# A matmul with a decayed running sum: one set of w's rows by another queue, ScalarE's order in the opening, and one PSUM bank

## The chip, the core and the metric

The kernel runs on one core of a Trainium2 chip. The core has TensorE (PE, matrix products into PSUM), VectorE (DVE), ScalarE (ACT), GpSimd (POOL) and SyncE (SP), and 16 DMA engines that all its DMA queues share. Each engine takes its instructions in the order in which the program gives them. The metric is device time in microseconds, the median over runs.

## The reference

x is [16, 2048, 1024], w is [1024, 1024], decay has 1024 values, all float32:

```python
xw = x @ w
out[:, 0, :] = xw[:, 0, :]
for t in range(1, S):
    out[:, t, :] = decay[None, :] * out[:, t - 1, :] + xw[:, t, :]
```

So there is one large product, and then along the sequence a linear recurrence for each batch and column.

## The kernel before

**Tiling.** The 16 sequences are cut into 64 chunks of 512 positions, and two neighbouring chunks make a group. The 1024 output columns are cut into 8 blocks of 128. The outer loop runs over groups, the inner one over blocks; one pass of the inner loop is a *slot*. Slots 0 to 7 are chunks 0 and 1 with blocks 0 to 7, slots 8 to 15 are chunks 2 and 3, and so on. A slot is 16 products of 128x128 with 128x512: k = 0 to 7 (the eight parts of the depth), for each of two chunks. Its result is two PSUM banks, columns on partitions and time along the free axis.

**PSUM.** There are eight banks. Three pairs, called `ps` 0 to 2, go round: slots 0, 1, 2 take them, then slots 4, 5, 6, then 7, 8, 9. Two single banks, `spare` and `spare1`, are used by slot 3, and after that not before the last group. A slot can only write its pair when the slot before on the pair has been emptied: slot 9 waits for slot 6.

**After the product** a slot takes one of two ways. Three of four are "paired": ScalarE copies the whole PSUM tile to SBUF (`copy`, line 183, a 128x1024 copy) and makes the decayed half of it (`odd`, line 169, `h<-ps`); GpSimd adds the two (`join`, line 196); VectorE scans half as many steps (line 201); ScalarE decays the result (`even`, line 169, `h<-so`) and GpSimd fills in the other half (`fill`, line 246). In the others VectorE scans PSUM directly (line 221). VectorE then transposes (line 258), and SyncE stores the result (line 282).

**x** is loaded by GpSimd's queue as bf16 (line 105), 32 rows at a time in four quadrants of a chunk, transposed by VectorE (`turn`, line 115) into `xw`, and put in order by a copy (`part`, line 123) into `xt`. A chunk's turn writes `xw`; its two ScalarE copies are called X (depth parts k = 0 to 3) and Y (k = 4 to 7).

**w** comes in four parts, (h, e): h is the half of the output columns, e says even or odd depth parts k. Part (0,0) is loaded as float32 by SyncE and ScalarE; the three others by GpSimd as bf16, four DMAs each, one per quadrant (`load_w`, line 299): U0 is part (0,1), U1 is (1,0), U2 is (1,1). A part has four row sets m = 0 to 3, and the row set m of part (h, e) is depth part k = 2m + e. The loaded rows are then copied into the stationary layout `wsb` (`settle`, line 306), one row set at a time: item number 8h + 4e + m. W is a settling by VectorE and w one by ScalarE.

**The order of the opening is written out by hand** in `agenda`, a list of letters with a number; key -99 stands ahead of slot 0, and the other keys follow the products of that slot. An engine's order is the order of its letters. p, g, z, j are copy, odd, zero and join of a slot; S is its scan; h, c, k are even, fill and the saving of its last column; B is the transpose back; L loads the next quadrant of x; T, X, Y turn and order a chunk; E, F, G do it for pieces of chunks 0 and 1; M loads them; D and d prepare decay and its square; K keeps TensorE going. So `p2` is ScalarE's copy of slot 2's tile, `w12` to `w15` are ScalarE's settling of part (1,1), and `j2` is GpSimd's join of slot 2.

In the opening the products of slots 0 to 3 are interleaved: for chunk 0 first the even k, then the odd ones. In slots 4 to 7 the even k come first too. Slots 8 and 9 are computed together: for chunk 2 slot 8's eight products, then slot 9's eight, and then the same for chunk 3, which reads `xw` directly. The pair of slot 9 is called `nexts`. The line numbers of the profile are those of this kernel:

Of the kernel before, what the change touches and what calls it, by code (L numbers as in the profile page):

```python
# [9 lines left out]
FP32 = mybir.dt.float32  # L10
# [4 lines left out]
def _ap(ap_obj: bass.AP, new_ap, extra_offset=0):  # L15
    return dataclasses.replace(
        ap_obj,
        ap=[list(p) for p in new_ap],
        offset=ap_obj.offset + extra_offset,
    )  # L20
# [5 lines left out]
def kernel(  # L26
# [26 lines left out]
    nc = tc.nc  # L53
    pin = tc.keep_in_program_order
    B, S, D = x.shape
    assert w.shape == (D, D)

    NQ = 4
    P = 32
    CQ = D // NQ  # L60
    K = CQ // P
    M = K // 2
    TL = 512
# [3 lines left out]
    CH = D // 2  # L67
    CR = CH // NQ

    const = ctx.enter_context(tc.tile_pool(name="const", bufs=1))  # L70
    sb = ctx.enter_context(tc.tile_pool(name="sb", bufs=1))
    psp = ctx.enter_context(tc.tile_pool(name="psp", bufs=1, space=bass.MemoryType.PSUM))
# [3 lines left out]
    def ring(pool, name, count, shape, dtype=FP32):  # L76
        i = turns[name] = turns.get(name, -1) + 1
        return pool.tile(shape, dtype, name=f"{name}{i % count}")

    def quad(q):  # L80
        return slice(q * P, (q + 1) * P)
# [7 lines left out]
    dec = const.tile([128, K], FP32, name="dec")  # L89
# [9 lines left out]
    xt_of = {}  # L99
# [25 lines left out]
    def matmul(ps, n, k, xt, t0=0, t1=TL, start=0, pairs=None):  # L125
        if pairs is None:
            rhs = xt[:, k // 2, k % 2, t0:t1]
        else:
            rhs = pairs[:, k // 2, t0 // P:t1 // P, :, k % 2].rearrange("p j i -> p (j i)")
        lhs = wsb[:, k, n].rearrange("p q i -> p (q i)")  # L130
        pin(nc.tensor.matmul(  # L131
            out=ps[:, t0:t1] if ps.shape[1] >= t1 else ps,
            lhsT=lhs,
            rhs=rhs,
            start=(k == 0 and t0 == start),
            stop=(k == K - 1),
        ))
# [3 lines left out]
    class Tile:  # L141
# [22 lines left out]
                self.held = sb.tile([128, 2 * TL + 2], FP32, name=f"so{self.turn % 4}")  # L164
            return self.held

        def decayed(self, src):
            h = ring(sb, "h", 4, [128, TL])[:, 0:self.T // 2]
            pin(nc.scalar.activation(  # L169
                out=h, in_=src, func=mybir.ActivationFunctionType.Copy,  # L170
                scale=dec[:, self.n:self.n + 1]))
            return h

        def pair(self):
            if self.paired:
# [4 lines left out]

        def copy(self):
            self.xs = sb.tile([128, 2 * TL], FP32, name=f"xs{self.lot % 3}")[:, 0:self.T]
            pin(nc.scalar.copy(out=self.xs, in_=self.ps))  # L183

        def odd(self):
            self.g = self.decayed(self.ps[:, 0:self.T:2])

        def zero(self):
            if self.prev is None:
# [8 lines left out]
        def scan(self):  # L198
            T, n, so = self.T, self.n, self.so
            if self.paired:  # L200
                pin(nc.vector.tensor_tensor_scan(  # L201
                    out=so[:, 3:T + 2:2],
                    data0=squares[-1][:, n:n + 1].to_broadcast([128, T // 2]),
                    data1=self.xs[:, 1:T:2],
                    initial=0.0 if self.prev is None else self.prev,
                    op0=ALU.mult,
                    op1=ALU.add,
                ))
            else:
                parts = self.ps if isinstance(self.ps, tuple) else (self.ps,)  # L210
                size = T // len(parts)
                for i, ps in enumerate(parts):
                    self.run(ps, i * size, size)

        def run(self, ps, t, size):
# [75 lines left out]
    size = M * CH  # L291
# [2 lines left out]
             (1, 0): room[1][:, 0:size // 2].bitcast(BF16),  # L294
             (1, 1): room[1][:, size // 2:size].bitcast(BF16)}

    def load_w(queues, h, e):
        for i, q in enumerate((0, 2, 1, 3)):
            pin(queues[i % len(queues)].dma_start(  # L299
                out=stage[h, e][quad(q)].rearrange("p (m d) -> p m d", m=M),  # L300
                in_=_ap(w, [[2 * D, P], [2 * P * D, M], [1, CH]],
                        (q * CQ + e) * D + h * CH)))

    def settle(h, e, m, copy):
        src = stage[h, e][:, m * CH:(m + 1) * CH]
        pin(copy(out=wcols[:, 2 * m + e, h],  # L306
                 in_=src.rearrange("p (q r i) -> p q r i", q=NQ, r=R)))

    idle = const.tile([128, TL], BF16, name="idle")
    spare = ring(psp, "spare", 1, [128, TL])  # L310
# [18 lines left out]
    for q in range(NQ):  # L329
        pin(nc.sync.dma_start(  # L330
            out=rows[q * P:q * P + R],
# [9 lines left out]
        spin(3 if q < NQ - 1 else 2, gates[q])  # L341

    def load_part(i):
        load_w((nc.gpsimd,), *((0, 1), (1, 0), (1, 1))[i])

    def part_one(i, copy):
        part(i // 8, copy, i % 4, i % 4 + 1, *halves[i // 4 % 2])
# [65 lines left out]
    def turn_and_load(c):  # L413
# [38 lines left out]
        "L": lambda i: load(*loads.pop(0)) if loads else None,  # L452
    }
    agenda = {
        -99: "M0 M1 U0 M2 M3 U1 U2 w0 W1 w2 W3 K0 K1 K2 K3 E0 E1 G0 E2 G1 E3 F2 G3 E4 E5 G4 E6 G5 E7 F6 G7 W4 w5 W6 W7 D E8 E9 G8 E10 G9 E11 F10 G11 E12 L E13 G12 L E14 G13 E15 L F14 G15",
        0: "p0 z0 W8 W9 W10 W11",
        1: "g0",
        2: "L S1 L",
        3: "p2 z2 L g2 j0 S3 w12 w13 L w14 L w15 k1",
        4: "j2 B1 d k3",  # L460
        5: "p4 L S0 L g4 S2 L k0 h0 j4 B3 h2",
        6: "k2 c0 T2 c2 p5 g5 B0 L X2 L",
# [85 lines left out]
    for step, (g, n) in enumerate(slots):  # L548
        T = TL * len(g)
        left = step - len(slots)  # L550
        if n % R == 0:
            ns, nj = range(n, n + R), T // P
            if left == -2 * R:
                outlets = [Outlet(ns, H, half) for half in range(2)]
            else:
                pieces = 1 if left < -7 * R else 2 if left < -6 * R else nj // H
                outlets = [Outlet(ns, nj, pieces=pieces)]
        if left == -R:
            outlets = []
        if step == 0:  # L560
            heads = [ring(psp, "ps", 3, [128, T]) for _ in range(3)]
            firsts = [ps[:, 0:TL] for ps in heads] + [spares[0]]
            seconds = [ps[:, TL:T] for ps in heads] + [spares[1]]
            for j0, j1 in halves:
                for k in range(0, K, 2):
                    for i in range(R):
                        matmul(firsts[i], i, k, xt_of[0], j0 * P, j1 * P, pairs=xw_of[0])
            for k in range(1, K, 2):
                for i in range(R):
                    matmul(firsts[i], i, k, xt_of[0])  # L570
            for k0 in range(0, K, 2):
                for i in range(R):
                    for k in (k0, k0 + 1):
                        matmul(seconds[i], i, k, xt_of[1], 0, H * P,
                               pairs=xw_of[1] if k0 < 4 else None)
            for i in range(R):
                for k in range(K):
                    matmul(seconds[i], i, k, xt_of[1], H * P, TL, H * P,
                           pairs=xw_of[1] if i < 2 else None)
        if step < R:  # L580
            ps = heads[n] if n < 3 else tuple(spares)
        else:
            if step == K + 1:
                ps = nexts
            elif len(g) == 2 or n % R < 3:
                ps = ring(psp, "ps", 3, [128, T])
            else:
                ps = ring(psp, "spare", 1, [128, TL])
            todo = [(k, l) for k in range(K) for l in range(len(g))]
            if step < K:  # L590
                todo.sort(key=lambda kl: kl[0] % 2)
            elif step == K:
                todo = []
                nexts = ring(psp, "ps", 3, [128, T])
                for l in range(len(g)):
                    for i, both in enumerate((ps, nexts)):
                        for k in range(K):
                            matmul(both[:, l * TL:(l + 1) * TL], n + i, k, xt_of.get(g[l]),
                                   pairs=xw_of[g[l]] if g[l] in (3,) else None)
            elif step == K + 1:  # L600
                todo = []
            if left == -1:
                ps = tuple(both[:, t:t + TL // 2] for t, both in zip(
                    (0, TL // 2), (ps, ring(psp, "ps", 3, [128, TL]))))
                blocks += [bank("spare1", 1), bank("ps", 3)]
                for t, half in zip((0, TL // 2), ps):
                    for k in range(K):
                        matmul(half, n, k, xt_of[g[0]], t, t + TL // 2, t)
                    if not t:
                        cross((1,), (0, 1))  # L610
                todo = []
            for k, l in todo:
                matmul(ps[:, l * TL:(l + 1) * TL], n, k, xt_of[g[l]])
        tiles.append(Tile(g, n, ps, outlets))
        do = agenda.get(step, agenda.get(left) if left >= -20 else None)
        if do is None:
            do = usual(step)
        else:
            do = do.split()
            if left == -20:  # L620
                do = rest(step) + do
        perform(do)
# [29 lines left out]
```

## Time and profile before

| | us |
|---|---|
| median of 3 runs | 904.99 (904.58 to 905.26) |
| span of the profiled execution, first to last instruction | 903.1 |
| median less span | 1.9 |
| TensorE busy (matmul) | 891.9, 99% of the span |
| VectorE busy | 825.6, 91% |
| ScalarE busy | 686.1, 76% |
| GpSimd busy | 657.1, 73% |
| granted TensorE clock, mean over the span | 1.000 |

In the answers of the trace, PE is TensorE's products and PEld its loads of the stationary operand. A line of a timeline has start, duration, engine, line, operation, what is written and read, shapes and a count; a bracket gives the idle time before it and what ended it. Neighbouring instructions of one kind are merged, so a line with x4 is four instructions. A matmul's record is longer than its share of TensorE, because products are pipelined: the distance from start to start is what one costs. Some matmul records are missing from the trace, so a step of two lengths is a missing record and no wait. A DMA's time to landing runs from its issue until all 16 engines have written their part.

### The profile page before, as it was taken

Reading aid. Unit: us, or ns where it says so; the run is one execution under the profiler, and the core shown is the slowest. Engines: PE = TensorE matmul, PEld = TensorE weight load, DVE = VectorE, ACT = ScalarE, POOL = GpSimd, SP = SyncE. Lnnn points to the kernel's source line nnn. Section 1 sums busy time; section 2 is a strip of 40 time slices with the busy share of each in tenths; the row PEclk is TensorE's granted clock in tenths of the full one; section 3 lists DMA queues with packets and bytes.
Section 4 is the critical chain, followed back from the end, with each engine's and each line's share of the span. In section 5 each row is a group of like instructions: output and inputs, shape, how many; then the busy total and the mean of one; then the engine's idle time right before and its main releaser. Section 6 shows DMA issues by size and latency. Waiting matters only on the chain.

```text
span 903.1 us, 12050 instructions
## 1 busy us (share of the span) xinstructions
PE 891.9 (99%) x4119; PEld 411.1 (46%) x4201; DVE 825.6 (91%) x632; ACT 686.1 (76%) x955; POOL 657.1 (73%) x755
## 2 busy tenths in 40 slices
PE   8999999999999999999999999999999999999998
PEld 5444444444444444444444444444444444444444
DVE  4999998999999999999998999999999999999998
ACT  4889867777877877878778778777787787787743
POOL 7888678777767768777677687777777776876632
PEclk9999999999999999999999999999999999999999
DMA  9999999999999999999999999999999999999858
GB/s 191 194 215 217 230 217 220 215 237 255 246 249 257 247 260 253 245 235 231 224 235 227 223 230 229 231 230 225 229 232 226 232 232 221 229 227 215 184 143 232
DMA packets 403182, 204.77 MB, mean 227 GB/s; under 512 B 9392, under 2 KB 402096, under 8 KB 403120
## 3 DMA queue, kind: packets, MB, share of 16 engines
q1 hardware_dynamic: 265808, 134.77, 61.0%
q0 software_dynamic: 137024, 68.70, 56.6%
q8 instruction: 33, 0.54, 0.2%
q10 hardware_dynamic: 288, 0.52, 0.2%
q14 instruction: 29, 0.24, 0.1%
HBM read 138.42 MB, written 134.22 MB: 302 GB/s over the span
## 4 chain that ended last, share of the span: by engine, by line
PE 94%; DMA 2%; POOL 1%; issue 1%; DVE 1%; ACT 0%; DVEq 0%; POOLq 0%
PE ps L131 94%; DMA xb<-in_x_dram 2%; POOL xb L105 1%; PE spare L131 1%; POOL ot L299 1%; DVE xw L115 0%; ACT xt L123 0%; DVE ot L258 0%; DVE so L201 0%; PE spare L384 0%; ACT xs L183 0%; PE ps L384 0%; DVE h L393 0%; ACT h L169 0%; DVEq L258 0%
## 5 line engine op out<-in xcount | busy, mean ns | idle before, releaser
L131 PE MATMUL ps<-xt,wsb 128*128 128x512 bf16 x3942 | 863.5, 378 | 4.6
L131 PEld LDWEIGHTS <-wsb 128*128 128x128 bf16 x4152 | 405.9, 98 | 479.8 <-ACT wsb L306 0.8
L196 POOL TENSOR_TENSOR xs<-h,xs 128x512 f32<-128x512 f32 (+1 forms) x190 | 243.0, 1279 | 189.3 <-ACT h L169 84.7
L183 ACT COPY xs<-ps 128x1024 f32<-128x1024 f32 (+1 forms) x190 | 189.3, 996 | 156.0 <-PE ps L131 145.7
L258 DVE STREAM_TRANSPOSE ot<-so 128x1024 f32<-128x1024 f32 (+2 forms) x264 | 300.2, 1175 | 2.3 <-POOL so L190 1.1
L246 POOL TENSOR_TENSOR so<-h,xs 128x512 f32<-128x512 f32 (+1 forms) x190 | 241.5, 1273 | 42.8 <-ACT h L169 27.9
L123 ACT COPY xt<-xw 128x2048 bf16<-128x2048 bf16 (+1 forms) x136 | 242.3, 1790 | 7.6 <-DVE xw L115 7.5
L105 POOL DMA_DIRECT2D xb<-in_x_dram x264 | 174.3, 661 | 2.9 <-DMA ot<-in_w_dram 1.0
L169 ACT ACTIVATE h<-so,dec 128x512 f32<-128x512 f32 (+1 forms) x190 | 145.3, 765 | 27.3 <-DVE so L201 24.1
L115 DVE STREAM_TRANSPOSE xw<-xb 128x2048 f32<-128x2048 f32 (+1 forms) x78 | 147.3, 1900 | 6.1 <-DMA xb<-in_x_dram 6.1
L201 DVE TENSOR_TENSOR_SCAN so<-spare,keep,xs 128x512 f32<-128x512 f32 (+1 forms) x97 | 119.9, 1239 | 27.4 <-POOL xs L196 27.1
L201 DVE TENSOR_TENSOR_SCAN so<-spare,xs 128x512 f32<-128x512 f32 x93 | 113.2, 1219 | 27.2 <-POOL xs L196 24.4
L169 ACT ACTIVATE h<-ps,dec 128x512 f32<-128x512 f32 (+1 forms) x190 | 130.2, 685 | 0.0
L221 DVE TENSOR_TENSOR_SCAN so<-dec,ps 128x1024 f32<-128x1024 f32 x34 | 76.8, 2260 | 1.0 <-ACT h L169 1.0
L221 DVE TENSOR_TENSOR_SCAN so<-dec,keep,ps 128x1024 f32<-128x1024 f32 (+1 forms) x35 | 75.9, 2170 | 0.1
L250 ACT COPY keep<-so 128x1 f32<-128x1 f32 x136 | 25.4, 189 | 9.5 <-DVE so L221 9.0
L192 ACT COPY so<-keep 128x1 f32<-128x1 f32 x97 | 18.4, 191 | 2.5 <-DVE ot L258 2.3
L131 PE MATMUL ps<-xw,wsb 128*128 128x256 bf16 (+1 forms) x68 | 11.2, 301 | 0.0
L190 POOL MEMSET so<- 128x1 f32 x93 | 10.7, 116 | 0.6 <-DVE ot L258 0.6
L131 PE MATMUL spare<-xt,wsb 128*128 128x512 bf16 (+1 forms) x48 | 10.0, 335 | 0.0
L299 POOL DMA_DIRECT2D ot<-in_w_dram x12 | 6.6, 546 | 3.8 <-DMA xb<-in_x_dram 2.5
L324 PE MATMUL spare<-idle 128*128 128x512 bf16 x22 | 6.6, 468 | 1.2 <-DVE idle L314 1.2
(37 smaller groups left out, 37.0 us busy)
## 6 DMA issues: line engine op xcount, KB each, us to landing
out_dram<-ot SPq DMA_DIRECT2D x236, 512.0 KB, 11.0
xb<-in_x_dram POOLq DMA_DIRECT2D x248, 256.0 KB, 7.8
out_dram<-ot SPq DMA_DIRECT2D x56, 128.0 KB, 2.6
xb<-in_x_dram POOLq DMA_DIRECT2D x16, 128.0 KB, 5.9
out_dram<-ot SPq DMA_DIRECT2D x8, 256.0 KB, 4.0
ot<-in_w_dram POOLq DMA_DIRECT2D x12, 128.0 KB, 5.1
out_dram<-xb SPq DMA_DIRECT2D x3, 256.0 KB
ot<-in_w_dram ACTq DMA_DIRECT2D x2, 256.0 KB, 5.2
```

The costliest lines, as they stand in the source:

```text
L105: pin(nc.gpsimd.dma_start(out=xb_of[c][quad(q), j0:j1], in_=_ap(x, [[D, P], [P * D, j1 - j0], [1, CQ]], (b * S + t0 + j0 * P) * D + q * CQ)))
L115: pin(nc.vector.transpose(out=dst.rearrange("p (m j i) -> p j m i", m=M, i=P)[:, j0:j1, m0:m1], in_=src.rearrange("p (j m c) -> p j m c", ...
L123: pin(copy(out=xt_of[c][:, m0:m1, :, j0 * P:j1 * P], in_=src))
L131: pin(nc.tensor.matmul(out=ps[:, t0:t1] if ps.shape[1] >= t1 else ps, lhsT=lhs, rhs=rhs, start=(k == 0 and t0 == start), stop=(k == K - 1),))
L169: pin(nc.scalar.activation(out=h, in_=src, func=mybir.ActivationFunctionType.Copy, scale=dec[:, self.n:self.n + 1]))
L183: pin(nc.scalar.copy(out=self.xs, in_=self.ps))
L196: pin(nc.gpsimd.tensor_tensor(out=odds, in0=self.g, in1=odds, op=ALU.add))
L201: pin(nc.vector.tensor_tensor_scan(out=so[:, 3:T + 2:2], data0=squares[-1][:, n:n + 1].to_broadcast([128, T // 2]), data1=self.xs[:, 1:T:2 ...
L221: pin(nc.vector.tensor_tensor_scan(out=so[:, t + 2:t + 2 + size], data0=dec[:, n:n + 1].to_broadcast([128, size]), data1=ps, initial=befor ...
L246: pin(nc.gpsimd.tensor_tensor(out=self.so[:, 2:T + 2:2], in0=self.h, in1=self.xs[:, 0:T:2], op=ALU.add))
L250: pin(nc.scalar.copy(out=self.keep, in_=self.so[:, self.T + 1:self.T + 2]))
L258: pin(nc.vector.transpose(out=outlet.ot[:, :, c0:c0 + P], in_=self.so[:, 2 + t0:2 + t0 + nj * P].rearrange("p (i t) -> p i t", t=P)))
```

## The change

There are three edits, all before 60 us.

1. A float32 tile `early` is added. GpSimd's four DMAs of part (0,1) load row sets 1 to 3 only. Behind the third of them GpSimd writes one column of `early` with a memset, and behind the fourth, in program order, SyncE loads row set 0 into `early` as float32, in four DMAs of 64 KB. Since they write the tile that the memset writes, they wait for it. `settle` of that row set (W4) reads `early`.
2. In the agenda W4 is moved up past F6 and G7; W5 goes to VectorE and w6 to ScalarE instead of w5 and W6. In step 3, w12 to w15 go ahead of p2, z2 and g2, and the two loads L that stood between them follow S3.
3. Slot 9 no longer takes both banks of its pair: its first chunk (chunk 2) goes to `spare`, its second to the second bank of the pair. Its tile is then two banks that don't adjoin, so copy and odd are made in two pieces.

```diff
-        def decayed(self, src):
+        def decayed(self, *srcs):
             h = ring(sb, "h", 4, [128, TL])[:, 0:self.T // 2]
-            pin(nc.scalar.activation(
-                out=h, in_=src, func=mybir.ActivationFunctionType.Copy,
-                scale=dec[:, self.n:self.n + 1]))
+            size = self.T // 2 // len(srcs)
+            for i, src in enumerate(srcs):
+                pin(nc.scalar.activation(
+                    out=h[:, i * size:(i + 1) * size], in_=src,
+                    func=mybir.ActivationFunctionType.Copy,
+                    scale=dec[:, self.n:self.n + 1]))
             return h
+
+        def parts(self):
+            return self.ps if isinstance(self.ps, tuple) else (self.ps,)
...
         def copy(self):
             self.xs = sb.tile([128, 2 * TL], FP32, name=f"xs{self.lot % 3}")[:, 0:self.T]
-            pin(nc.scalar.copy(out=self.xs, in_=self.ps))
+            size = self.T // len(self.parts())
+            for i, ps in enumerate(self.parts()):
+                pin(nc.scalar.copy(out=self.xs[:, i * size:(i + 1) * size], in_=ps))
 
         def odd(self):
-            self.g = self.decayed(self.ps[:, 0:self.T:2])
+            size = self.T // len(self.parts())
+            self.g = self.decayed(*[ps[:, 0:size:2] for ps in self.parts()])
...
+    early = const.tile([128, CH], FP32, name="early")
+
-    def load_w(queues, h, e):
+    def load_w(queues, h, e, m0=0):
         for i, q in enumerate((0, 2, 1, 3)):
             pin(queues[i % len(queues)].dma_start(
-                out=stage[h, e][quad(q)].rearrange("p (m d) -> p m d", m=M),
-                in_=_ap(w, [[2 * D, P], [2 * P * D, M], [1, CH]],
-                        (q * CQ + e) * D + h * CH)))
+                out=stage[h, e][quad(q)].rearrange("p (m d) -> p m d", m=M)[:, m0:],
+                in_=_ap(w, [[2 * D, P], [2 * P * D, M - m0], [1, CH]],
+                        (q * CQ + e + 2 * P * m0) * D + h * CH)))
+            if m0 and i == NQ - 2:
+                pin(nc.gpsimd.memset(early[:, 0:1], 0.0))
+
+    def load_early():
+        for q in range(NQ):
+            pin(nc.sync.dma_start(
+                out=early[quad(q)],
+                in_=_ap(w, [[2 * D, P], [1, CH]], (q * CQ + 1) * D)))
 
     def settle(h, e, m, copy):
-        src = stage[h, e][:, m * CH:(m + 1) * CH]
+        src = early if (h, e, m) == (0, 1, 0) else stage[h, e][:, m * CH:(m + 1) * CH]
...
     def load_part(i):
-        load_w((nc.gpsimd,), *((0, 1), (1, 0), (1, 1))[i])
+        load_w((nc.gpsimd,), *((0, 1, 1), (1, 0), (1, 1))[i])
+        if i == 0:
+            load_early()
...
-        -99: "... E7 F6 G7 W4 w5 W6 W7 D E8 ..."
+        -99: "... E7 W4 F6 G7 W5 w6 W7 D E8 ..."
...
-        3: "p2 z2 L g2 j0 S3 w12 w13 L w14 L w15 k1",
+        3: "w12 w13 w14 w15 p2 z2 L g2 j0 S3 L L k1",
...
-                nexts = ring(psp, "ps", 3, [128, T])
+                nexts = (ring(psp, "spare", 1, [128, TL]), ring(psp, "ps", 3, [128, T])[:, TL:T])
                 for l in range(len(g)):
-                    for i, both in enumerate((ps, nexts)):
+                    for i, one in enumerate((ps[:, l * TL:(l + 1) * TL], nexts[l])):
                         for k in range(K):
-                            matmul(both[:, l * TL:(l + 1) * TL], n + i, k, xt_of.get(g[l]),
+                            matmul(one, n + i, k, xt_of.get(g[l]),
                                    pairs=xw_of[g[l]] if g[l] in (3,) else None)
```

## The prediction

> **What bounds the kernel now.** The page comes first: which engine is busy, and when.
>
> ```profile
> PE 891.9 (99%) x4119; PEld 411.1 (46%) x4201; DVE 825.6 (91%) x632; ACT 686.1 (76%) x955; POOL 657.1 (73%) x755
> ```
>
> TensorE sets the time, so the change can win only what TensorE waits. In the timeline 512-wide products start 0.216 us apart; from 41.67 to the tail they do so without a gap. I went through TensorE's timeline before that for longer steps. Four remain after the first real product at 11.08: 0.20 us at 13.10, 0.31 at 15.22, 0.02 at 28.85 and 0.29 at 41.67. Two of them, from narrow windows (a step is the difference of starts):
>
> ```profile
> 14.80 0.27 PE L131 MATMUL spare<-xw,wsb 128*128 128x256 bf16 x1
> 15.22 0.82 PE L131 MATMUL ps<-xt,wsb 128*128 128x512 bf16 x2
> ...
> 40.95 0.59 PE L131 MATMUL ps<-xt,wsb 128*128 128x512 bf16 x2
> 41.67 0.38 PE L131 MATMUL ps<-xt,wsb 128*128 128x512 bf16 x1
> ```
>
> At 14.80 a 256-wide product starts; its successor could start at 14.91 and starts at 15.22. At 41.16 the second of the pair starts; its successor comes 0.51 later instead of 0.22. VectorE's row shows the first reason (w's first odd row set lands late), the chain of waits the second (slot 6's bank must be emptied for slot 9):
>
> ```profile
> 14.86 0.88 DVE L306 COPY wsb<-ot 128x512 bf16<-128x512 bf16 x3 [0.53 <-DMA ot<-in_w_dram]
> ```
>
> ```profile
> 38.22 1.89 ACT xt L123
> 40.12 0.91 ACT xs L183
> 41.03 0.60 ACT h L169
> 41.63 0.04 issue
> 41.67 6.58 PE ps L131 x29
> ```
>
> The change aims at these three steps: 0.31 + 0.02 + 0.29 = 0.62 us is the most it can win. It moves work on ScalarE, so its timeline and GpSimd's are the next views:
>
> ```profile
> 24.26 0.69 ACT L169 ACTIVATE h<-ps,dec 128x512 f32<-128x512 f32 x1
> 25.13 1.01 ACT L183 COPY xs<-ps 128x1024 f32<-128x1024 f32 x1 [0.18 <-PE ps L131]
> 26.04 0.69 ACT L169 ACTIVATE h<-ps,dec 128x512 f32<-128x512 f32 x1
> 26.62 2.17 ACT L306 COPY wsb<-ot 128x512 bf16<-128x512 bf16 x4
> ...
> 34.67 1.01 ACT L183 COPY xs<-ps 128x1024 f32<-128x1024 f32 x1 [0.71 <-POOL so L246]
> 35.58 0.69 ACT L169 ACTIVATE h<-ps,dec 128x512 f32<-128x512 f32 x1
> 36.42 3.70 ACT L123 COPY xt<-xw 128x2048 bf16<-128x2048 bf16 x2
> ```
>
> ```profile
> 20.53 0.54 POOL L299 DMA_DIRECT2D ot<-in_w_dram  x1 [0.19 <-issue]
> ...
> 28.90 1.30 POOL L196 TENSOR_TENSOR xs<-h,xs 128x512 f32<-128x512 f32 x1
> 30.14 1.94 POOL L105 DMA_DIRECT2D xb<-in_x_dram  x3
> 32.09 1.30 POOL L196 TENSOR_TENSOR xs<-h,xs 128x512 f32<-128x512 f32 x1
> 33.34 2.54 POOL L246 TENSOR_TENSOR so<-h,xs 128x512 f32<-128x512 f32 x2
> ```
>
> GpSimd has no gap from 28.90 to 35.9: j2, three loads, j4, c0, c2. ScalarE's p5 (34.67) waited for c0 (33.34 to 34.63). The row at 20.53 issues the last load of w's last part (U2); the DMA view of that moment gives its landing:
>
> ```profile
> ot<-in_w_dram POOLq DMA_DIRECT2D x1, 128.0 KB, 5.6
> ```
>
> 20.53 + 5.6 = 26.13 us. Today that is hidden: ScalarE is in p2 and g2 until 26.62.
>
> **The first row set by SyncE.** GpSimd's four loads U0 shrink from four row sets to three; a memset (0.12 by the L190 row) goes behind the third. That issue ends near 10.3 (9.12 + two of the three in 1.77), so SyncE issues at 10.4 to 11.9 (0.37 each: four decay loads took 1.49). SyncE has nothing else until 38.66, so nothing queues there. Landing of the last, 64 KB: between 11.5 + 2.6 (128 KB stores) and 11.5 + 4.7 (256 KB loads by SyncE), 14.1 to 16.2; I take 14.1, nearest in size. W4 now stands ahead of F6 on VectorE, behind E7 (ends 14.02), and casts float32: 0.42 (first L306 rows). It ends at 14.6, before 14.91, and the 0.31 goes. At 16.2 it would end at 16.7: 1.5 later than today, with F6, W5 and W7 behind it. Next due is E8 (17.68 to 18.13) for the product at 18.69 - 0.31 = 18.38: free.
>
> The bytes are the larger price. The windows move 203 GB/s into SBUF in w's cast loads (11.5 to 13.5) and 306 in its first, plain ones (2.5 to 4.5). Freed: 131 KB at 203, 0.64 us; added: 262 KB at 306, 0.86. All that lands behind, U2 too, comes 0.22 later. Bounds: -0.64 (SyncE's bytes cost nothing) and +0.65 (they move at 203).
>
> [...]
>
> **w12 to w15 ahead of p2.** Nothing is added; order changes. g0 ends at 24.95, and w12 must now wait for U2: 26.13 + 0.1 (w5 starts 0.1 after U0's landing) = 26.24 instead of 26.62, so w15 ends 0.38 earlier, at 28.41. TensorE, 0.31 earlier, wants it at 28.52: the step at 28.85 stays away. But ScalarE stands idle 1.3 us with p2 and g2 behind the wait, whose input is ready at 25.1. w15 starts 1.55 after w12; then 0.52, p2 0.91, g2 0.69 (starts in the rows): g2 ends at 26.24 + 3.67 = 29.91, not 26.73. j2 needs it: 29.99 instead of 28.90, **1.09 later**. Since GpSimd has no gap, c0 ends at 35.72, p5 starts at 35.75. g5 follows 0.91 later, then 0.58 to X2: 37.24 instead of 36.42 (X2 waited for T2 until 36.38, which hides 0.26). Y2 starts 1.81 later and takes 1.89: ends **40.95** instead of 40.12.
>
> Y2 feeds slot 8's fifth product. Slot 8 starts eight products before 41.38, at 39.65, so today the fifth comes at 40.52, 0.40 after Y2. With 0.33 won it wants Y2 at 40.18 and starts at 41.00: a new wait of 0.82.
>
> VectorE hardly sees it: S2 (31.87) needs j2, now done at 31.3; the transpose at 37.44 needs c2, done at 36.97. The three loads after j2 feed chunk 4, transposed at 48.5: hidden.
>
> **Slot 9's first chunk in the spare bank.** Slot 3's scan of that bank ends at 28.31 (27.13 + 1.19): free. The 0.29 at 41.67 goes; slot 9's second chunk needs slot 6's bank only at 45.4, emptied near 42.5. Copy and odd product of slot 9 become two each: by starts, 0.52 x 2 for 0.91, and about 0.36 x 2 for 0.58, so 0.26 us more on ScalarE near 50. By bank releases against slot starts, slot 11 has 1.42 us today and slot 16 1.12; ScalarE and VectorE 0.8 later and TensorE 0.2 later leave some 0.6. Without that cover they cost 0.26.
>
> **Sum.** Won: 0.31 + 0.02 + 0.29 = 0.62. New: 0.82. With U2 as now: +0.20; with U2 0.22 later: **+0.41 us**. While Y2 governs, it absorbs what TensorE gains earlier, one for one. The profiled span is 903.1, the median 904.99, so 1.9 lies around it: 903.5 in a span, 905.4 as a median.
>
> **Rivals.**
> - *The new wait stays away.* If U2 lands 0.82 us sooner (25.3), Y2 is no limit and all 0.62 is won: 904.4. For it: that landing took 5.6 us where w's loads have a median of 5.1. Against: SyncE's added bytes. Between, U2 half a microsecond sooner gives 904.7. Chance 0.27 for anything faster than now.
> - *The float32 load is late.* Landing at 16.2, W4 costs TensorE 1.5 at 15.22; it then comes to slot 8's fifth product at 42.0, past Y2, and only the 0.29 is won: +1.2, 906.2. For it: SyncE's loads took 4.7. Against: those were four times as large. 0.10.
> - *Slower beyond what can be told.* A measurement of this kernel tells about 0.2%, 1.8 us. ScalarE's queue stops at w12, so each microsecond that U2 is late is one at the end; it decides from U2 1.6 late (27.7), giving 906.8 and more. For it: the last load of w's part before, issued at 17.84, took 6.0. Against: 1.6 is over twice the upper bound of the bytes. 0.08.
> - *It doesn't do what it says*: slot 9's first chunk still waits, with Y2 past: the time is then set by Y2 as above or by the bank near 42.5, 905.4 to 906. 0.05.
>
> **How the numbers follow.** The forecast, Y2 in place of three short waits (904.9 to 905.8 by the bounds that keep Y2 the limit), has the remaining 0.50. Range 904.4 to 906.1: it takes in the full win and leaves out the upper tail and part of the late loads. No case reaches 1.8 us faster: 0.02 for what I don't see. Slower by over 0.2%: 0.08 and 0.02 of late loads. Within: 0.88.
>
> **What the profile would show.** Right: no step at 15.22; ScalarE idle before the four L306 copies, named DMA, starting at 26.2 to 26.5; GpSimd waiting for L169 before its second L196; a step of TensorE near 41 ended by ACT L123; none from slot 8 to 9. Wrong: U2 landing before 25.5, GpSimd with a gap ahead of c0, or W4 ending after 15.2.

## The result, and the profile after

The changed kernel takes 906.63 us (median of 7 executions, 906.35 to 908.59); the kernel before takes 904.99 in the same comparison (7 executions, 904.58 to 905.26). The ratio is 1.0024, with an interval of 1.0014 to 1.0033: slower by 1.64 us, where 0.4 was forecast, and above the range (906.1). The profiled execution is the 908.59 one, with a span of 906.8 against 903.1 before. It carries 1.7 us that most executions don't have; where these come from is said below.

The page of the changed kernel shows the same load on every engine, to within 1 us but for TensorE:

```profile
PE 897.9 (99%) x4201; PEld 411.6 (45%) x4201; DVE 826.2 (91%) x632; ACT 685.6 (76%) x957; POOL 656.6 (72%) x756
```

So nothing large was added (82 of TensorE's 4201 products had no record before, and some now run at half clock), and again the question is where TensorE waits. Its timeline (start, duration, operation, then the idle time before it and what ended that), first at the change from even to odd products, then at slots 8 and 9:

```profile
14.41 0.27 PE L131 MATMUL spare<-xw,wsb 128*128 128x256 bf16 x1
17.11 0.82 PE L131 MATMUL ps<-xt,wsb 128*128 128x512 bf16 x3 [2.43 <-DVE wsb L324]
...
19.22 1.48 PE L131 MATMUL ps<-xt,wsb 128*128 128x512 bf16 x3
...
37.80 7.29 PE L131 MATMUL ps<-xt,wsb 128*128 128x512 bf16 x33
44.92 1.46 PE L131 MATMUL spare<-xt,wsb 128*128 128x512 bf16 x6
```

The first odd product, which started at 15.22 before, starts at 17.11; its predecessor's place ends at 14.52, so the step that was 0.31 us is now 2.59. From slot 8 into slot 9, in the last two lines, there is no step. TensorE comes there some 3 us later than before, so this trace alone doesn't say that the moved bank took the step away; the bank's own experiment below does. VectorE's, SyncE's and ScalarE's timelines give the reason and what became of the rest:

```profile
16.63 0.43 DVE L324 CAST wsb<-early 128x512 bf16<-128x512 f32 x1 [2.99 <-DMA early<-in_w_dram]
```

```profile
10.15 1.72 SPq L318 DMA_DIRECT2D early<-in_w_dram  x4
```

```profile
26.93 1.01 ACT L191 COPY xs<-ps 128x1024 f32<-128x1024 f32 x1 [3.95 <-PE ps L131]
27.83 0.69 ACT L171 ACTIVATE h<-ps,dec 128x512 f32<-128x512 f32 x1
28.41 2.17 ACT L324 COPY wsb<-ot 128x512 bf16<-128x512 bf16 x4
30.48 1.02 ACT L191 COPY xs<-ps 128x1024 f32<-128x1024 f32 x1
...
39.42 3.70 ACT L123 COPY xt<-xw 128x2048 bf16<-128x2048 bf16 x2
```

SyncE issues its four loads from 10.15 to 11.86, as forecast. VectorE then stands idle 2.99 us until the last of them has landed, and W4 runs from 16.63 to 17.06. ScalarE's copies of w's end do not wait for U2 here (it landed at 26.93): ScalarE comes to them at 28.41, because TensorE gave it its earlier work late. Y2 ends at 43.12, 3.00 later than before; TensorE wants it at about 44.06, so the forecast wait for Y2 does not occur. The chain of work that ended last, in order of time, runs through the new load:

```profile
10.01 0.12 POOL early L314
...
11.44 5.06 DMA early<-in_w_dram
...
16.63 0.44 DVE wsb L324
17.06 0.05 issue
17.11 0.82 PE ps L131 x3
```

The fourth load, 64 KB, is issued at 11.44 and lands 5.06 us later; the four took 3.4, 4.5, 4.9 and 5.1. The last view is the table by stretches of 2 us (busy time and instructions of PE, PEld, DVE, ACT, POOL, then the granted clock, the DMA share and GB/s):

```profile
16.00:18.00 2.00, 0.89 (x5) 0.42 (x6) 1.34 (x6) 0.00 (x0) 1.50 (x3) 1.00 1.43 192
18.00:20.00 2.00, 2.00 (x7) 0.72 (x6) 1.96 (x7) 1.16 (x3) 1.60 (x4) 0.62 1.42 196
20.00:22.00 2.00, 2.00 (x6) 0.73 (x5) 1.26 (x5) 1.19 (x3) 1.67 (x4) 0.53 1.24 202
22.00:24.00 2.00, 2.00 (x18) 1.58 (x17) 0.57 (x2) 0.97 (x2) 1.67 (x4) 1.00 1.23 202
```

After the pause the clock is at half for some 3.4 us. From 18.46 to 21.88 eight products start 0.427 apart instead of 0.216, which costs 8 x 0.211 = 1.69 us. The profiled execution and one other (908.39) have a mean clock of 0.998 and lie 1.4 to 2.2 above the other five, 906.35 to 907.0, at 0.999 to 1.000. That all of this gap in the second is the half clock is inferred from its mean (3.41 us at half speed in 907 lower it by 0.0019).

The account of the profiled execution, by starts of TensorE's products: the first odd product 1.89 later (17.11 for 15.22), half clock 1.69, slot 9's step gone, -0.29, the step at 28.85 gone, -0.02: 3.27. TensorE's last product starts 3.26 later (901.64 for 898.38), and the tail of stores is 0.47 longer: 3.73, and the spans differ by 3.7. Without the half clock and that tail, 1.58 is left; the medians differ by 1.64.

### The profile page after: what moved, and what is told of

It is laid out like the page before. It is cut to its first block, busy times and chain, and to the rows that moved or that the text cites. A ratio compares the mean times of both kernels' runs of the same rounds, so it can differ in the third digit from the quotient of the medians.

```text
span 906.8 us, 12141 instructions
## 1 busy us (share of the span) xinstructions
PE 897.9 (99%) x4201; PEld 411.6 (45%) x4201; DVE 826.2 (91%) x632; ACT 685.6 (76%) x957; POOL 656.6 (72%) x756
## 4 chain that ended last, share of the span: by engine, by line
PE 98%; DMA 1%; POOL 0%; issue 0%; SPq 0%; DVE 0%; DVEq 0%; POOLq 0%
PE ps L131 96%; PE spare L131 1%; DMA xb<-in_x_dram 1%; DMA early<-in_w_dram 1%; SPq L318 0%; POOL ot L309 0%; PE spare L404 0%; PE ps L404 0%; POOL xb L105 0%; DVE h L413 0%; DVE wsb L324 0%; POOL early L314 0%; DVEq L324 0%; POOLq L656 0%
## 5 line engine op out<-in xcount | busy, mean ns | idle before, releaser
L131 PE MATMUL spare<-xt,wsb 128*128 128x512 bf16 (+1 forms) x56 | 12.4, 350 | 0.0
```

Source lines behind the costliest of these rows:

```text
L131: pin(nc.tensor.matmul(out=ps[:, t0:t1] if ps.shape[1] >= t1 else ps, lhsT=lhs, rhs=rhs, start=(k == 0 and t0 == start), stop=(k == K - 1),))
```

## The experiments

Two theories. A: SyncE's load lands too late, and that is the loss. B: ScalarE's order is the loss, by the chain through Y2 that the prediction worked out. The first four kernels each hold a part of the change (the kernel before: 904.99, 33 executions). The diffs show the lines that matter; `...` marks what is left out.

**All but the load by SyncE.** Row set 0 comes with GpSimd's loads as before; order and bank are the changed ones. The diff is against the changed kernel.

```diff
-        load_w((nc.gpsimd,), *((0, 1, 1), (1, 0), (1, 1))[i])
-        if i == 0:
-            load_early()
+        load_w((nc.gpsimd,), *((0, 1), (1, 0), (1, 1))[i])
...
-        -99: "... E7 W4 F6 G7 W5 w6 W7 D E8 ..."
+        -99: "... E7 F6 G7 W4 w5 W6 W7 D E8 ..."
```

> The changed kernel with part (0,1) of w again whole by GpSimd's queue and W4 in its old place; ScalarE's new order and slot 9's bank stay. Theory A, the SyncE load alone is the loss (it landed at 16.51, W4 was late, TensorE stood 2.6 us): the loss is gone. With the prediction's Y2 wait on top: ScalarE idle until U2 lands near 26.1, Y2 ending near 40.95, a TensorE step of about 0.5 us ended by it, none at slot 9: 0.2 us slower than before. Without any Y2 wait: 0.3 us faster. Theory B, ScalarE's order is the loss: 1.5 us slower or more.

Measured: 905.07, ratio 1.0001 (0.9992 to 1.0010). Without the load the loss is gone, so theory A holds. Whether Y2's wait costs the 0.2 us that were expected can't be told: the interval holds that and nothing. In its profile ScalarE now does wait for U2, and GpSimd's join behind it for ScalarE (it starts at 30.34, g2 ends at 30.26), as the prediction said:

```profile
26.59 2.18 ACT L314 COPY wsb<-ot 128x512 bf16<-128x512 bf16 x4 [0.96 <-DMA ot<-in_w_dram]
28.67 1.00 ACT L191 COPY xs<-ps 128x1024 f32<-128x1024 f32 x1
...
37.60 3.70 ACT L123 COPY xt<-xw 128x2048 bf16<-128x2048 bf16 x2
```

Y2 ends at 41.30, and TensorE steps only 0.20 there, because in this execution it lost 0.63 at the odd products and is itself later.

**The load by SyncE alone**, with W4 moved up and W5 and w6 on their new engines: the order of step 3 and slot 9's bank are those of before. The diff is against the changed kernel.

```diff
-        3: "w12 w13 w14 w15 p2 z2 L g2 j0 S3 L L k1",
+        3: "p2 z2 L g2 j0 S3 w12 w13 L w14 L w15 k1",
...
-                nexts = (ring(psp, "spare", 1, [128, TL]), ring(psp, "ps", 3, [128, T])[:, TL:T])
+                nexts = ring(psp, "ps", 3, [128, T])
...
```

> The kernel before with the SyncE load of row set 0 and W4 moved up, nothing else. Theory A: the same late landing (16 to 17 us), a step of about 2.6 us of TensorE before the odd products of chunk 0, and 1.4 to 2 us slower than before, more in executions in which the clock drops. Theory B: within 0.3 us of before.

Measured: 906.36, ratio 1.0017 (1.0008 to 1.0026), +1.37. TensorE's timeline and VectorE's:

```profile
14.89 0.27 PE L131 MATMUL spare<-xw,wsb 128*128 128x256 bf16 x1
16.72 0.82 PE L131 MATMUL ps<-xt,wsb 128*128 128x512 bf16 x2 [1.55 <-DVE wsb L324]
```

```profile
16.24 0.43 DVE L324 CAST wsb<-early 128x512 bf16<-128x512 f32 x1 [2.12 <-DMA early<-in_w_dram]
```

The load alone makes the step (16.72 - 15.00 = 1.72, before 0.31: 1.41 more) and with it nearly all of the loss. One of its 11 executions took 908.81, with a mean clock of 0.997. There is no step at slot 9 in its trace either, though the bank is not moved: a TensorE that is late by more than 0.29 us doesn't wait for slot 6's bank.

**Slot 9's bank alone**, against the kernel before.

```diff
-                nexts = ring(psp, "ps", 3, [128, T])
+                nexts = (ring(psp, "spare", 1, [128, TL]), ring(psp, "ps", 3, [128, T])[:, TL:T])
...
```

> The kernel before with slot 9's first chunk in the spare bank, nothing else. The step of 0.29 us at slot 9 is gone and nothing takes its place: 0.3 us faster. If the two extra pieces on ScalarE were not hidden: 0 to 0.3 us slower than that.

Measured: 904.91, ratio 0.9998 (0.9989 to 1.0006). TensorE from slot 8 into slot 9:

```profile
37.68 3.83 PE L131 MATMUL ps<-xt,wsb 128*128 128x512 bf16 x17
41.35 1.89 PE L131 MATMUL spare<-xt,wsb 128*128 128x512 bf16 x8
```

Slot 9 starts at 41.35 without a step, where before its place was at 41.38 and it started at 41.67: here TensorE is not late, so it is the moved bank that took the step away. In this execution the step at the odd products is 0.63 instead of 0.31, which uses the gain up. The time says neither -0.3 nor 0: the interval holds both.

**ScalarE's order alone**, against the kernel before.

```diff
-        3: "p2 z2 L g2 j0 S3 w12 w13 L w14 L w15 k1",
+        3: "w12 w13 w14 w15 p2 z2 L g2 j0 S3 L L k1",
```

> The kernel before with w12 to w15 ahead of p2, nothing else. By the prediction's chain (U2 at 26.1, g2 ending near 29.9, j2 1.1 us later, Y2 ending near 40.95, slot 6's bank emptied near 42.5): a step of 0.4 to 0.5 us at slot 8's fifth product and one of 0.6 at slot 9 in place of 0.29: 0.8 us slower. If the chain has slack that the prediction missed: no change, within 0.1 us.

Measured: 905.92, ratio 1.0009 (1.0000 to 1.0018), +0.93, at the edge of what can be told. The profiled execution is the slowest of the 11 (906.77). ScalarE's timeline and TensorE's show the chain link by link:

```profile
26.66 2.18 ACT L314 COPY wsb<-ot 128x512 bf16<-128x512 bf16 x4 [1.70 <-DMA ot<-in_w_dram]
...
36.19 1.01 ACT L191 COPY xs<-ps 128x1024 f32<-128x1024 f32 x1 [1.77 <-POOL so L254]
37.09 0.69 ACT L171 ACTIVATE h<-ps,dec 128x512 f32<-128x512 f32 x1
37.68 3.70 ACT L123 COPY xt<-xw 128x2048 bf16<-128x2048 bf16 x2
```

```profile
41.42 1.02 PE L131 MATMUL ps<-xt,wsb 128*128 128x512 bf16 x4 [0.71 <-ACT xt L123]
42.93 1.24 PE L131 MATMUL ps<-xt,wsb 128*128 128x512 bf16 x5 [0.48 <-ACT h L171]
```

ScalarE waits for U2 until 26.6, p5 waits for c0, Y2 ends at 41.38, and TensorE waits for it (a step of 0.87); slot 9's bank, not moved here, costs another 0.64 behind it. So B's mechanism is real; alone it is worth 0.9 us by the medians, with an interval of 0 to 1.6. In the whole change it is covered by A, since a TensorE that is late by more than Y2 doesn't wait for Y2.

The next question was whether the load can be had in time, and what the half clock costs (before: 905.01, 13 executions).

**Without the memset** that holds SyncE's issue back, against the changed kernel.

```diff
-            if m0 and i == NQ - 2:
-                pin(nc.gpsimd.memset(early[:, 0:1], 0.0))
```

> The changed kernel without the memset, so that SyncE issues the four float32 loads right behind decay's, near 3.1 us instead of 10.1. If the lateness is that of the issue (held back by GpSimd's memset), row set 0 lands before 10 us, W4 runs right behind E7 near 14.1, the step of 2.6 us is gone; x's first quadrants share the DMA engines with 262 KB more and chunk 0 comes 0.3 to 0.9 us later: 905.0 to 905.8, some 1 us faster than the changed kernel. If any load on SyncE's queue lands some 6 us after its issue and costs as much wherever it is put, x comes so much later that nothing is won: 906.4.

Measured: 908.20, ratio 1.0037 (1.0023 to 1.0051), against both expectations. SyncE issues at 5.33, 5.70, 7.38 and 7.74, and not from 3.1: in the trace the four loads use the completion semaphores of w's first four loads again, and each is issued only when that one has landed (5.31, 5.05, 7.37, 6.97). They land by 13.41, so W4 is in time, but now something else is late:

```profile
14.55 0.50 PE L131 MATMUL ps<-xw,wsb 128*128 128x256 bf16 x3 [1.37 <-DVE xw L115]
```

That is x's second half of chunk 0, landed at 13.93 where before the change it came at 12.47 (in the changed kernel at 12.09). U2 lands at 29.10, 2.2 later than in the changed kernel, and costs steps of 0.85 at 29.87 and, through Y2, 0.86 at 43.95. With the 1.53 at 14.55 these are most of the added time. The 1.5 us of x are near what 256 KB take at the 196 GB/s that were moved from 5 to 8.5 us (1.3 us, an estimate from this trace); why U2 is late by over 2 stays open.

**Row set 0 first, by GpSimd itself**: its own four small loads ahead of the other three row sets, w12 to w15 between p2 and g2, the bank moved. The diff is against the changed kernel; the last two arguments of `load_w` are the first row set and the one behind the last.

```diff
-        load_w((nc.gpsimd,), *((0, 1, 1), (1, 0), (1, 1))[i])
+        load_w((nc.gpsimd,), *((0, 1, 0, 1), (1, 0), (1, 1))[i])
         if i == 0:
-            load_early()
+            load_w((nc.gpsimd,), 0, 1, 1)
...
-        3: "w12 w13 w14 w15 p2 z2 L g2 j0 S3 L L k1",
+        3: "p2 z2 L w12 w13 w14 w15 g2 j0 S3 L L k1",
```

> No SyncE load: GpSimd loads row set 0 of part (0,1) by four DMAs of its own (bf16) ahead of the other three row sets. W4 stays ahead of F6; step 3 is p2, then w12 to w15, then g2; slot 9's first chunk in the spare bank. By the theory that the queue and the moment were the loss: row set 0 lands near 13.2, no step at the odd products; p2 covers ScalarE's wait for U2, g2 ends near 29.0, Y2 where it was; steps at 28.85 and slot 9 gone: 0.4 to 0.6 us faster than before. If the four additional DMAs hold up x (each DMA of GpSimd waits for the landing of the eighth before it): 0 to 0.5 us slower.

Measured: 907.23, ratio 1.0024 (1.0015 to 1.0034), slower than both expectations. The first odd product starts at 14.86 without a step, but TensorE stops behind it:

```profile
16.88 0.82 PE L131 MATMUL ps<-xt,wsb 128*128 128x512 bf16 x3 [1.00 <-DVE wsb L314]
...
20.32 0.84 PE L131 MATMUL ps<-xw,wsb 128*128 128x256 bf16 x6 [0.68 <-DVE xw L115]
```

The other row sets land at 16.41 (before 14.74), and x's loads behind them are issued from 13.26 instead of 10.87: in the trace GpSimd's loads use eight completion semaphores in turn, and each is issued only when the eighth before it has landed (in the trace of the kernel before the ninth is issued at 8.15, the first having landed at 7.87, and the tenth at 9.12 behind the second's 8.83), so four more of them push all that follow.

**The load later still, and the pause filled.** The first kernel moves memset and load behind the issue of x's next loads (M2); the second also lets TensorE do 16 products on data that nobody uses while it waits. The diff is against the changed kernel.

```diff
-        if i == 0:
-            load_early()
...
+        if i == 2:
+            pin(nc.gpsimd.memset(early[:, 0:1], 0.0))
+            load_early()
...
+            for _ in range(16):
+                pin(nc.tensor.matmul(out=spares[1], lhsT=idle[:, 0:128], rhs=idle, start=True, stop=True))
```

> The changed kernel with memset and SyncE load behind the third half of x (M2), some 3 us later. If the landing follows the issue, it comes near 19.5 and TensorE stands 5 to 6 us instead of 2.6: by that alone 3 us slower than the changed kernel in its full-clock executions. If a pause of TensorE lowers its clock (the changed kernel's profile has 3.4 us at half clock 1.4 us after its pause), the stretch at half clock is in every execution now and adds 1.7 us: 911 in all. If the low clock is chance and not the pause's: 909.5.

> The same late load, with 16 idle products (3.5 us, results unused, into slot 3's second bank before it is needed) for TensorE to work on while it waits. If the pause lowers the clock, the stretch at half clock is gone and the kernel 1.5 to 2 us faster than the one without idle products. If something else lowers it: the same time and clock as that one.

Measured: 913.41, ratio 1.0092 (1.0078 to 1.0106), and 910.35, ratio 1.0067 (1.0052 to 1.0083). The first lands later than its expectation had it (21.74 for 19.5) and takes longer by that. Its TensorE and then the stretches:

```profile
15.41 0.27 PE L131 MATMUL spare<-xw,wsb 128*128 128x256 bf16 x1
22.35 1.46 PE L131 MATMUL ps<-xt,wsb 128*128 128x512 bf16 x3 [6.66 <-DVE wsb L322]
```

```profile
18.00:20.00 2.00, 0.00 (x0) 0.00 (x0) 0.00 (x0) 0.00 (x0) 0.77 (x3) 0.59 1.13 162
...
22.00:24.00 2.00, 1.65 (x4) 0.58 (x5) 1.92 (x9) 0.00 (x0) 2.00 (x4) 0.50 1.24 202
24.00:26.00 2.00, 2.00 (x8) 0.84 (x7) 2.00 (x7) 1.83 (x4) 1.96 (x5) 0.70 1.24 202
```

With this pause of 6.8 us half clock came in all four executions (mean clock 0.995 to 0.996), here from 18.37 to 25.20. The second, filled, in the same views:

```profile
14.59 3.61 PE L588 MATMUL spare<-idle 128*128 128x512 bf16 x16
20.20 0.82 PE L131 MATMUL ps<-xt,wsb 128*128 128x512 bf16 x3 [1.99 <-DVE wsb L322]
```

```profile
22.00:24.00 2.00, 2.00 (x12) 1.01 (x11) 2.00 (x7) 2.00 (x4) 2.00 (x3) 1.00 1.26 208
```

Here a pause of 2.15 us is left (18.05 to 20.20) and the clock stays full, as it does in three of its four executions by their mean clocks (0.999; the fourth has 0.997). The difference between the two is not the clock's alone. Of the 3.6 us between the spans of the profiled executions 2.15 are the later first odd product (22.35 for 20.20) and 1.42 the half clock from there to 25.20. The load landed at 19.60 in the second and 21.74 in the first; it was issued 0.93 later in the first, in which all loads ran later from x's first quadrant on (landed at 8.43 for 7.43). Of the rest I know no cause.

Then, what makes the landing take 5 us (before: 904.98, 21 executions).

**One load of 256 KB instead of four of 64**, against the changed kernel.

```diff
-        for q in range(NQ):
-            pin(nc.sync.dma_start(
-                out=early[quad(q)],
-                in_=_ap(w, [[2 * D, P], [1, CH]], (q * CQ + 1) * D)))
+        pin(nc.sync.dma_start(
+            out=early,
+            in_=_ap(w, [[CQ * D, NQ], [2 * D, P], [1, CH]], D)))
```

> The changed kernel with row set 0 in one DMA of 256 KB on SyncE's queue in place of four of 64 KB. If the lateness is four small DMAs one behind the other (they landed 3.4, 4.5, 4.9 and 5.1 us after issues at 10.15 to 11.4), the one lands near 14 us, 4 us after its issue, and the step before the odd products shrinks from 2.6 to some 0.3: 904.8 to 905.3. If the lateness is the sharing of the 16 DMA engines with GpSimd's backlog, 262 KB stay 262 KB: landing at 15.5 to 16.5, 906 to 906.6.

Measured: 912.59, ratio 1.0082 (1.0068 to 1.0096): far outside both.

```profile
19.59 0.43 DVE L323 CAST wsb<-early 128x512 bf16<-128x512 f32 x1 [5.65 <-DMA early<-in_w_dram]
```

The load landed at 19.50, 8.3 us after its issue ended, and x's eight loads behind it took 8.6 to 8.8 us to land. In the trace it has 4 completions, where each load of 64 KB has 16; why it has 4 is not shown. TensorE stood for 5.19 us, and half clock came with it (17.41 to 24.23; a mean clock of 0.995 to 0.997 in all five executions): 4.88 us more of pause and 2.07 of clock make up nearly all of the 7.0 us between the spans. So the one load differs from the four in its completions too, and the run doesn't answer the question it was made for.

**A quarter of the bytes.** Four loads of 16 KB; the other three quarters of row set 0 are zeros, a part of w that is left out. The diff is against the changed kernel.

```diff
-                out=early[quad(q)],
-                in_=_ap(w, [[2 * D, P], [1, CH]], (q * CQ + 1) * D)))
+                out=early[quad(q), 0:CH // 4],
+                in_=_ap(w, [[2 * D, P], [1, CH // 4]], (q * CQ + 1) * D)))
...
+    pin(nc.vector.memset(early, 0.0))
```

> The changed kernel with a quarter of the columns in SyncE's four loads (16 KB each); three quarters of row set 0 stay zero, so that part of w is left out of the product. If bytes and sharing set the landing, the last lands 1.5 to 3 us sooner (13.5 to 15) and the step shrinks to under 1 us: 904.6 to 905.4. If it is a fixed time for each DMA, it lands at 16 as before: 906.3.

Measured: 905.99, ratio 1.0011 (1.0001 to 1.0021). The summary line of the loads' tile, and TensorE:

```profile
DMA to landing us min/median/max: 3.4/4.0/4.1
```

```profile
16.24 0.82 PE L131 MATMUL ps<-xt,wsb 128*128 128x512 bf16 x2 [1.17 <-DVE wsb L324]
```

The time lies between the two expectations. The last load lands at 15.64, 4.09 us after its issue instead of 5.06: three quarters of the bytes are worth 1.0 us. That is what 192 KB take at the 203 GB/s of the prediction's window (0.97, an estimate). The other 4 us are not the load's own bytes; it is late even when it is small.

**Bank moved, w12 to w15 between p2 and g2, no load by SyncE**: what is left of the change without the late load and with half of the order. The diff is against the changed kernel and leaves out the removal of the load.

```diff
-        3: "w12 w13 w14 w15 p2 z2 L g2 j0 S3 L L k1",
+        3: "p2 z2 L w12 w13 w14 w15 g2 j0 S3 L L k1",
```

> No SyncE load; the kernel before with slot 9's first chunk in the spare bank and step 3 as p2, w12 to w15, g2. p2 covers ScalarE's wait for U2 (26.1 to 26.6), w15 ends 0.2 to 0.4 us sooner than before, g2 ends near 29 to 29.3, Y2 0.0 to 0.2 later and still ahead of its use: no step at 28.85, 41 or slot 9; 0.3 us faster than before, 904.7. If ScalarE's queue stands at w12 longer than p2 covers, Y2 becomes late as in the kernel with w12 ahead of p2: 905.0 to 905.3.

Measured: 904.77 (904.36 to 905.33), ratio 0.9997 (0.9988 to 1.0006). Its trace has no step at 28.85, at 41 or at slot 9, but 0.2 us can't be told from nothing here.

**x's next loads held back** until the early load has landed, by a GpSimd copy that reads it; the diff is against the changed kernel (before: 904.85, 4 executions).

```diff
             load_early()
+            pin(nc.gpsimd.tensor_copy(out=seen, in_=early[:, 0:1]))
```

> The changed kernel with a GpSimd copy of one column that reads the SyncE load, placed ahead of x's third half (M2): GpSimd's following loads are issued only when row set 0 has landed. If the 5.1 us of the last SyncE load are the sharing with GpSimd's backlog of x, it lands 1 to 2 us sooner (14 to 15.2; issue at 10.1 to 11.5). If they are the load's own (issue, first packet, write), it lands at 16 to 16.5 as before. Either way chunk 1 of x comes some 4 us late, TensorE waits for it near 18, and the kernel is 3 to 6 us slower than before.

Measured: 910.67, ratio 1.0069 (1.0046 to 1.0092).

```profile
15.51 0.43 DVE L325 CAST wsb<-early 128x512 bf16<-128x512 f32 x1 [1.42 <-DMA early<-in_w_dram]
```

```profile
DMA to landing us min/median/max: 4.0/4.2/4.5
```

With x's next loads out of the way the last landing comes at 15.39 instead of 16.51; the fourth still takes 4.0 us from its issue. So these loads are 1.1 of the 5.1 us. What GpSimd issued ahead of the load is still there: at 11.38, when the fourth is issued, chunk 0's last two quadrants (landing at 11.80 and 12.54) and all of U0 (12.97 to 14.77) are under way. The view of the DMA engines from 10 to 12 us shows GpSimd's queue (q0) alone, its packets' times adding up to more than the 16 engines' time:

```profile
DMA packets 686, 0.39 MB, mean 197 GB/s; under 512 B 53, under 2 KB 686, under 8 KB 686
...
q0 software_dynamic: 686, 0.39, 138.3%
```

SyncE's first load is issued at 10.08, its first packet starts at 12.30, and the last packet of the four ends at 14.83. So by this trace most of the 4.0 us goes by while the engines work on what was issued before. No run has the load with the engines idle, so how much would be left is not shown. W4 is still late (a step of 1.02), and the hold makes chunk 1 late (a step of 4.19 at 23.65); these two are most of the time lost. In the profiled execution half clock comes on top (22.20 to 29.03).

## Why the prediction was wrong

**The step that failed** is the landing of SyncE's last load: "between 11.5 + 2.6 (128 KB stores) and 11.5 + 4.7 (256 KB loads by SyncE), 14.1 to 16.2; I take 14.1, nearest in size". It landed at 16.51, 5.06 us after its issue began. The prediction let the load's bytes delay what lands behind them, but left out that the load itself lands behind what GpSimd had issued before it. The row was chosen by size, and size was the wrong thing to be near in: 16 KB loads took up to 4.1 us, and 64 KB ones 4.0 to 4.5 with x held back. Rows nearer in kind or moment said more. SyncE's loads (4.7) were the other end of the bound, and nearly right; x's loads that GpSimd issued at 10.87 and 11.61 before the change took 4.56 and 4.57. Taking the 4.7 would have given the second rival, priced 906.2 with a chance of 0.10, and that rival is what happened: removing the load removes the loss, and the load alone brings 1.37 of the 1.64 us. W4 ended at 17.06, which the prediction had named as a sign of being wrong (after 15.2).

That the change is slower, as forecast, is luck: the wait for Y2 that was to make it so doesn't occur in the changed kernel.

**Its own terms, one by one.**
- Issue at 10.4 to 11.9: measured 10.15 to 11.86. W4 as a float32 cast, 0.42: 0.43. The memset, 0.12: 0.12. All right.
- The 0.31 at the odd products: not won; the step is 2.59. The rival's price for a late load, 1.5, was short of the 1.89 by which the first odd product is later; 0.31 of this is the landing past the bound (16.51 for 16.2).
- U2 0.22 later by the added bytes: not resolved. It landed at 26.93 in the changed kernel and 26.57 with the load alone; without the load at 26.06 to 26.56 in five traces (26.15 in the one of before). That the bytes cost time at all was the author's assumption, which no run had shown when the prediction was made. The kernel without the memset, where the same 256 KB early in the stream come with x 1.5 us later (13.93 for 12.47) and U2 by more (29.10 for 26.15), agrees with it.
- w12 to w15 ahead of p2: the chain was right in every link. Alone it costs 0.93 (0 to 1.6) where 0.8 was expected. Y2's end is 41.38 for the 40.95 worked out, in a trace in which U2 landed 0.41 later. In the whole change the wait doesn't appear, because it is TensorE that is late.
- "While Y2 governs, it absorbs what TensorE gains earlier, one for one": no run tests a gain, but a loss of 1.89 is larger than Y2's 0.82, and then Y2 governs no more. The rival had this.
- Slot 9's bank: the bank alone takes the step of 0.29 away in its trace. In the changed kernel the step is gone too, but so it is with the load alone, where the bank isn't moved. That the bank makes the time shorter isn't measured: alone it gave 0.08, with the smaller change of order 0.21, both below what the comparisons can tell.
- The clock was left out altogether. A pause was priced as its own length. In 2 of 7 executions (the second by its mean clock) the 2.59 us pause was followed by 3.41 us at half clock, 1.69 us more in the trace.

**What stays open:** how long SyncE's 64 KB take to land when the DMA engines are idle; why U2 is over 2 us later in the kernel without the memset; and whether a kernel with the bank and the smaller change of order beats the one before: 904.77 against 904.98 doesn't say so.

## What to carry to other kernels

Price a landing by rows of the same kind, queue and moment, not of the same size, and ask what was issued ahead of it: here a quarter of the bytes took four fifths of the time, and a load that had 0.3 us to spare by the one row was 1.5 us too late by the other. When a change both delays TensorE and delays what TensorE waits for, only the larger counts, so take the parts apart before concluding that the smaller one costs nothing, or that a step which is gone was won. A pause of TensorE cost more than its length here (2.59 us of pause, and 1.69 more by half clock behind it, in the profiled execution); look at the granted clock behind one.

## What the runs showed of the hardware that was not expected

- The half clock with a pause lasted 3.41 us (18.46 to 21.88) after 2.59 us of pause, and 6.83 with pauses of 4.19 (x held back), 5.19 (one load) and 6.82 (the load later still). It began 3.94 us after the start of the shortest, when products had been running again for 1.35, and 2.5 to 2.9 after the start of the others. It came with the 2.59 us pause in 2 of 7 executions, with those of 5.19 and 6.82 in all, and with one of 1.7 (the load alone) in 1 of 11 by its mean clock.
- One DMA of 256 KB had 4 completions in the trace and not 16, and landed at 19.50, 3 us later than the same bytes as four DMAs; loads of GpSimd issued behind it took 8.6 to 8.8 us.
- With part of the wait filled by products that nobody uses, the clock stayed full in three of four executions; unfilled, in none of four (1.00 against 0.50 granted from 22 to 24 us). As the landing differed too, the filling isn't shown to be the only reason.
